# One layer of a chunked hybrid trunk: a shorter mLSTM norm, the bias column negated on ScalarE, and the decay additions queued behind another chunk's norm sum

## The chip, the core and the metric

The kernel runs on one core of a Trainium2 chip. The core has a matrix engine (TensorE, PE in the profile, with its weight loads shown apart as PEld), three engines for elementwise work (VectorE = DVE, ScalarE = ACT, GpSimd = POOL), a queue for data transfers (SyncE = SP) and 16 DMA engines. Each engine takes its instructions in the order of its own queue; an instruction that has to wait holds those behind it. The metric is the time of one execution on the device in microseconds; the median of several runs is compared.

## The reference

One layer over 2048 tokens of width 1024, all in float32. After an RMS norm and one wide projection, three groups of heads work side by side: chunked softmax attention with a relative bias, mLSTM, and gated linear attention (GLA). Their outputs are gated, joined, projected back, added to the input and normalised. What matters here is the end of mLSTM, whose rows are divided by a denominator and then normalised per head, and the relative bias of attention:

```python
# mLSTM, per chunk
d_mat = jnp.exp(log_d - m_row[..., None])            # the decay
sc = jnp.einsum('bnthd,bnjhd->bnhtj', qc, kc) * d_mat
...
den = jnp.maximum(jnp.abs(den), jnp.exp(-m_row))
out = num / den.transpose(0, 1, 3, 2)[..., None]
...
# per head, over 64 columns
y = xf * lax.rsqrt(jnp.mean(xf * xf, axis=-1, keepdims=True) + EPS)
```

## The kernel before

The 2048 tokens are worked off in four quarters of 512 tokens (`q`). In each quarter PE runs the projections: a tile is 24 matmuls of 128x512 into one of two PSUM banks named `ip` (lines L240 to L242 and L260 to L262), which ScalarE or VectorE then evict (L507 to L519, L585 and L586, L490 and L496, and others). Every weight tile arrives by DMA in `wraw` and is split into a high and a low part, by ScalarE (L231) and by VectorE or GpSimd in turn (L232). Between the projections PE does the small matmuls of mLSTM and GLA. After the four quarters (from about 900 us) comes attention with the output projection.

The order of PE's instructions is written out by hand: `Flow` steps through the generators `gates`, `mlstm`, `gla_in`, `gla` and others while the projections run, and each `yield` says how many microseconds of other matmul work should pass before the next step. The order on all other engines is planned by the program that builds the kernel: it simulates the engines and takes, on each, the instruction of highest priority that is ready by its simulation. Evictions and weight splits have a raised priority. The order is then fixed, and on the chip each engine follows it whatever is ready.

A step of `mlstm` is a chunk of 128 tokens, four in a quarter, 16 in all:

- The decay. `load_dd` (L651) loads a row of numbers to all partitions into `dd`, which has two buffers; the load of chunk c+1 is issued in step c and waits for the buffer of chunk c-1. Six additions on VectorE (L665, one for each head, capped by a mask) and one exponential on ScalarE (L667) make the decay.
- The scores. PE multiplies keys by queries (L672), VectorE multiplies by the decay (L684), and PE multiplies by the values (L695).
- The chunk's output, `ov`, is put together on VectorE (L698, L701), with the denominator in column 64 of each head; the state `Cbd` is updated (L716).
- The norm. ScalarE squares the output (L719), VectorE sums the squares (L721) into `sm[:, 0]` and makes the denominator in `sm[:, 1]` (L722 to L724). A reciprocal on VectorE (L725) and five instructions on GpSimd (L726 to L730, the fourth a power of -1/2) make the factor `sm[:, 3]`, all on tiles of 128x6.
- VectorE multiplies the output by the factor (L733), PE transposes it (L631, in `mlstm_out`), and VectorE applies the gate (L633). In the last quarter the transposes of the first three chunks are held back.

GLA has a norm of its own with a power on GpSimd (L892, L893, L895), and a product L853 (after L850) for which PE waits at L860.

`bias_rel`, called once in quarter 1, loads the bias table's last column (L615, `bc`), negates it on VectorE (L616) and adds it to the table `bt` of each of six heads on ScalarE (L619).

Of the kernel before, what the change touches and what calls it, by code (L numbers as in the profile page):

```python
# [1 line left out]

# [8 lines left out]
AF = mybir.ActivationFunctionType  # L11
ALU = mybir.AluOpType
# [12 lines left out]
EPS = 1e-6  # L25
# [80 lines left out]
def trunk_kernel(ctx: ExitStack, tc: tile.TileContext, xT, x, w_f, w_t, w_o, w_gates, norm_g, conv_w,  # L106
                 gate_sel, one_row, bias, ml_g, gla_g, final_g, out):
    nc = tc.nc
# [19 lines left out]
    mhalf = const.tile([P, 16], FP32, name="mhalf")  # L128
# [18 lines left out]
    with ExitStack() as pa_:  # L147
# [13 lines left out]
        def d_tile():  # L161
            return big.tile([P, 6, L], FP32, name="dd", bufs=2)
# [14 lines left out]
        cap = one.tile([P, L], FP32, name="cap")  # L177
# [435 lines left out]
        def bias_rel():  # L613
            bc = big.tile([P, AH], FP32, name="sm")
            nc.sync.dma_start(bc, bias[:, :, 256])  # L615
            nc.vector.tensor_scalar(bc, bc, -1.0, None, op0=ALU.mult)  # L616
            nc.sync.dma_start(bt, bias[:, :, 0:256])
            for h in range(AH):
                nc.scalar.activation(bt[:, h, :], bt[:, h, :], AF.Identity, bias=bc[:, h:h + 1])  # L619
            nc.gpsimd.memset(bt[0:64, :, 192:256], NEG)  # L620
# [24 lines left out]
        def mlstm(q, qk, vs, R, held=None):  # L645
            rt, iwl = R["rt"], R["iwl"]
            if held is not None:
                hbs = [xraws.tile([P, D], FP32, name="xraw") for _ in range(3)][0::2]
            def load_dd(c):
                dd = d_tile()  # L650
                nc.sync.dma_start(dd, nm_d[q, :, c * L:(c + 1) * L].partition_broadcast(P))  # L651
                return dd

            nxt = load_dd(0)
            for c in range(NC):
                t0 = q * QT + c * L
# [4 lines left out]
                dd = nxt  # L661
                if c + 1 < NC:
                    nxt = load_dd(c + 1)
                for e in range(6):
                    nc.vector.scalar_tensor_tensor(dd[:, e, :], dd[:, e, :], rt[:, c, 0, e:e + 1], cap,  # L665
                                                   op0=ALU.add, op1=ALU.min)
                nc.scalar.activation(dd, dd, AF.Exp)  # L667
                yield 0.0, 9.0 if c == 0 else 3.5
                sps = [bank("s", 2) for _ in range(2)]
# [26 lines left out]
                if not first:  # L696
# [3 lines left out]
                                            op=ALU.mult)  # L700
                    nc.vector.tensor_tensor(oc, ov, oc, op=ALU.add)  # L701
                    ov = oc
                if t0 + L < S:
# [5 lines left out]
                    for b in range(2):  # L709
                        r = slice(64 * b, 64 * b + 64)  # L710
                        for a in range(3):
# [3 lines left out]
                            else:  # L715
                                nc.vector.scalar_tensor_tensor(dst, dst, iwl[r, 3 * b + a, c:c + 1], cv[r, a, :],  # L716
                                                               op0=ALU.mult, op1=ALU.add)
                sq = m_tile([P, 2, 3, 64])
                nc.scalar.activation(sq, ov[:, :, :, 0:64], AF.Square)  # L719
                sm = big.tile([P, 4, 2, 3], FP32, name="sm")  # L720
# [1 line left out]
                nc.vector.tensor_scalar(sm[:, 1], ov[:, :, :, 64], -1.0, None, op0=ALU.mult)  # L722
                nc.vector.tensor_tensor(sm[:, 1], sm[:, 1], rt[:, c, 2, :].rearrange("p (b a) -> p b a", b=2), op=ALU.max)
                nc.vector.tensor_tensor(sm[:, 1], ov[:, :, :, 64], sm[:, 1], op=ALU.max)  # L724
                nc.vector.reciprocal(sm[:, 1], sm[:, 1])  # L725
                nc.gpsimd.tensor_tensor(sm[:, 2], sm[:, 1], sm[:, 1], op=ALU.mult)  # L726
                nc.gpsimd.tensor_tensor(sm[:, 2], sm[:, 2], sm[:, 0], op=ALU.mult)
                nc.gpsimd.tensor_scalar(sm[:, 2], sm[:, 2], 1.0 / 64, EPS, op0=ALU.mult, op1=ALU.add)
                nc.gpsimd.tensor_tensor(sm[:, 2], sm[:, 2], mhalf[:, 0:6].rearrange("p (b a) -> p b a", b=2), op=ALU.pow)
                nc.gpsimd.tensor_tensor(sm[:, 3], sm[:, 2], sm[:, 1], op=ALU.mult)  # L730
                late_ = held is not None and c < NC - 1
                hb = m_tile([P, 3, 2, 64]) if held is None else hbs[c // 2][:, 512 * (c % 2):512 * (c % 2) + 384].rearrange("p (a b d) -> p a b d", a=3, b=2)
                nc.vector.tensor_tensor(hb.rearrange("p a b d -> p b a d"), ov[:, :, :, 0:64],  # L733
# [173 lines left out]
        for q in range(NQ):  # L907
# [3 lines left out]
            if q == NQ - 1:  # L911
                z = proj_z(X)
                G, gh, mh = {}, [], []
                tail = proj_v(X)
                vs, vg = next(tail)
                flow.start("gla_in", gla_in(q, z, R, G))
                flow.need("mlstm")
                qk = proj_m(X)
                flow.need("gates")
                st["per"] = 2  # L920
                M = dict(R)
                flow.start("mlstm", mlstm(q, qk, vs, M, mh))
                flow.start("mlstm_out", held_out(q, mh, M))
                gg = proj_gg(X)
                next(tail)
                flow.start("gla", gla(q, vg, gg, G, gh))
                flow.start("gla_out", held_gla(q, lambda: gg, gh))
                M["gm"] = proj_gm(X)
                proj_a(q, X)
                break  # L930
# [12 lines left out]
            if q == 1:  # L943
                bias_rel()
            M = dict(R)
            flow.start("mlstm", mlstm(q, qk, vs, M))
            M["gm"] = proj_gm(X)
            R = {}
# [391 lines left out]
```

## Time and profile before

| | us |
|---|---|
| median of 3 runs | 1302.21 (1302.17 to 1312.29) |
| the profiled execution | 1304.63 |
| its span, first to last instruction | 1302.5 |

The median is that of three executions without the profiler. The profiled execution is another one; all rows are of it, in microseconds from its first instruction. A row of the timeline has start, duration, engine, line, operation, output and inputs by their names in the program, shape, and in brackets the idle time of that engine just before, with the instruction that ended it. A row of waits names who waited for whom, the sum, how often, and the longest. A row of a stretch has, for each engine, busy time and number of instructions, then the granted clock of TensorE (1.00 is full speed), the share of time in which the DMA engines were busy, and the rate of transfers in GB/s.

### The profile page before, as it was taken

The page shows a single profiled execution, that of the slowest core. Times are in us where ns is not written, and L with a number is a line of the kernel's source. Part 1 is how long each engine was busy: PE and PEld are TensorE (multiplying, and loading weights), DVE is VectorE, ACT ScalarE, POOL GpSimd, SP SyncE. Part 2 cuts the span into 40 slices and gives each one's busy share as a digit, 9 for nine tenths or more (in the row PEclk, how much of TensorE's full clock was granted, in tenths as well). Part 3 has the DMA queues.
Part 4 walks back from the last instruction along what each step waited for, and adds up shares of the span by engine and source line. Part 5 has one row for each costly group of instructions (what it writes and reads, how often), then busy time and mean ns, then how long its engine had stood idle before and what let it go on. Part 6 is the DMA issues. An engine that isn't in the chain of part 4 may idle for free.

```text
span 1302.5 us, 19360 instructions
## 1 busy us (share of the span) xinstructions
PE 1254.7 (96%) x6804; PEld 1021.0 (78%) x6804; DVE 800.8 (61%) x1838; ACT 590.2 (45%) x1096; POOL 604.3 (46%) x825
## 2 busy tenths in 40 slices
PE   8989999999999999999999999999988999999997
PEld 7867877878787788878778877787867878878876
DVE  6646645772575668267476766664567677666631
ACT  5536332453533236353323643332565566655631
POOL 3337663233766243375533455652354454554432
PEclk8989999999999999999999999999989999999999
DMA  6147344424733442473344242426785565655322
GB/s 226 57 135 255 98 140 128 119 55 139 255 97 111 124 128 72 138 254 92 113 126 126 75 135 89 131 59 191 231 231 188 184 191 161 190 173 176 97 90 81
DMA packets 100185, 184.34 MB, mean 142 GB/s; under 512 B 10592, under 2 KB 46304, under 8 KB 100088
## 3 DMA queue, kind: packets, MB, share of 16 engines
q1 hardware_dynamic: 95624, 174.98, 43.2%
q10 hardware_dynamic: 4464, 8.13, 1.7%
q8 instruction: 53, 0.87, 0.3%
q14 instruction: 44, 0.36, 0.1%
HBM read 147.38 MB, written 35.70 MB: 141 GB/s over the span
## 4 chain that ended last, share of the span: by engine, by line
PE 72%; DVE 9%; DMA 7%; POOL 4%; ACT 3%; issue 3%; SPq 0%; POOLq 0%; DVEq 0%; ACTq 0%
PE ip L240 10%; PE ip L242 10%; PE ip L241 10%; PE ip L1192 4%; PE ip L1194 4%; PE ip L1193 4%; PE s L1051 3%; PE ip L260 3%; PE tp L1111 3%; PE ip L262 3%; PE ip L261 3%; DMA wraw<-in_w_f 2%; DMA dd<-nm_d 2%; PE ga L843 2%; PE w L1130 2%
## 5 line engine op out<-in xcount | busy, mean ns | idle before, releaser
L240 PE MATMUL ip<-x,w 128*128 128x512 f32 x784 | 321.4, 410 | 1.4 <-ACT u L551 1.4
L242 PE MATMUL ip<-x,w 128*128 128x512 f32 x784 | 308.3, 393 | 0.0
L241 PE MATMUL ip<-x,w 128*128 128x512 f32 x784 | 307.4, 392 | 0.0
L240 PEld LDWEIGHTS ip<-x,w 128*128 128x128 f32 x784 | 148.5, 189 | 43.3 <-issue 11.7
L242 PEld LDWEIGHTS ip<-x,w 128*128 128x128 f32 x784 | 148.0, 189 | 32.7
L241 PEld LDWEIGHTS ip<-x,w 128*128 128x128 f32 x784 | 148.8, 190 | 29.3 <-issue 1.9
L231 ACT CAST w<-wraw 128x1024 fp32r<-128x1024 f32 x126 | 131.6, 1046 | 64.9 <-DMA wraw<-in_w_f 33.5
L232 POOL TENSOR_TENSOR w<-wraw,w 128x1024 fp32r<-128x1024 f32 x42 | 103.9, 2473 | 111.7 <-ACT w L231 111.6
L232 DVE TENSOR_TENSOR w<-wraw,w 128x1024 fp32r<-128x1024 f32 x84 | 111.3, 1325 | 64.6 <-ACT w L231 64.5
L1072 POOL TENSOR_SCALAR pt<-pt,sm 128x640 f32<-128x640 f32 (+2 forms) x96 | 71.4, 746 | 112.2 <-DVE sm L1071 90.2
L260 PE MATMUL ip<-w,x 128*128 128x512 f32 x256 | 104.3, 407 | 8.2 <-DVE e L496 5.5
L262 PE MATMUL ip<-w,x 128*128 128x512 f32 x256 | 101.3, 396 | 0.0
L261 PE MATMUL ip<-w,x 128*128 128x512 f32 x256 | 101.1, 395 | 0.0
L1070 ACT ACTIVATE pt<-pt,sm 128x640 f32<-128x640 f32 (+2 forms) x96 | 73.2, 763 | 47.1 <-DVE sm L1067 43.4
L786 POOL TENSOR_TENSOR prd<-gk,zg 128x16 f32<-128x16 f32 (+7 forms) x112 | 66.5, 594 | 58.6 <-PE pw L792 53.3
L1118 DVE TENSOR_TENSOR pl<-tp,ph 128x512 fp32r<-128x512 f32 (+1 forms) x108 | 71.9, 673 | 33.1 <-ACT ph L1117 32.8
L1051 PE MATMUL s<-kk,qq 128*128 128x256 f32 (+2 forms) x360 | 83.8, 318 | 7.6 <-DVE sm L1067 2.8
L1051 PEld LDWEIGHTS s<-kk,qq 128*128 128x128 f32 x360 | 63.5, 192 | 22.7 <-DVE sm L1067 7.6
L783 POOL TENSOR_TENSOR gk<-gk,al 128x16 f32<-128x16 f32 (+14 forms) x120 | 70.8, 590 | 21.3 <-ACT al L760 14.3
L1117 ACT CAST ph<-tp 128x512 fp32r<-128x512 f32 (+1 forms) x108 | 60.5, 572 | 42.2 <-PE tp L1111 41.5
L560 DVE SCALAR_TENSOR_TENSOR qk<-u,cw,qk 128x512 f32<-128x512 f32 x72 | 68.4, 950 | 13.7 <-ACT qk L558 12.1
L1201 POOL TENSOR_TENSOR xr<-xr,e 128x512 f32<-128x512 f32 x31 | 40.1, 1293 | 60.8 <-ACT jk L1199 60.5
(345 smaller groups left out, 2481.6 us busy)
## 6 DMA issues: line engine op xcount, KB each, us to landing
wraw<-in_w_f SPq DMA_DIRECT2D x100, 512.0 KB, 3.7
wraw<-in_w_t SPq DMA_DIRECT2D x28, 512.0 KB, 3.7
qq<-q_d SPq DMA_DIRECT2D x48, 256.0 KB, 4.9
kk<-k_d SPq DMA_DIRECT2D x18, 512.0 KB, 6.3
vv<-v_d SPq DMA_DIRECT2D x18, 512.0 KB, 5.9
xraw<-in_xT SPq DMA_DIRECT2D x16, 512.0 KB, 6.1
xr<-in_x SPq DMA_DIRECT2D x16, 512.0 KB, 3.6
out<-xr ACTq DMA_DIRECT2D x31, 256.0 KB, 2.6
```

The costliest lines, as they stand in the source:

```text
L231: nc.scalar.copy(w[:, :, 0, :], rv)
L232: other().tensor_tensor(w[:, :, 1, :], rv, f32(w[:, :, 0, :]), op=ALU.subtract)
L240: nc.tensor.matmul(ps, w[:, k, 0, :], X[k][:, 0, :], start=(k == 0), stop=False)
L241: nc.tensor.matmul(ps, w[:, k, 0, :], X[k][:, 1, :], start=False, stop=False)
L242: nc.tensor.matmul(ps, w[:, k, 1, :], X[k][:, 0, :], start=False, stop=(k == KT - 1))
L260: nc.tensor.matmul(ps, X[k][:, 0, t], w[:, 0, :], start=(k == 0), stop=False)
L261: nc.tensor.matmul(ps, X[k][:, 0, t], w[:, 1, :], start=False, stop=False)
L262: nc.tensor.matmul(ps, X[k][:, 1, t], w[:, 0, :], start=False, stop=(k == KT - 1))
L1051: nc.tensor.matmul(sp[:, :cn], qq[:, l, tt * P:(tt + 1) * P], kk[:, ko + c0:ko + c0 + cn], start=(l == 0), stop=(l == 1))
L1070: nc.scalar.activation(pt[:, :n], pt[:, :n], AF.Exp, bias=init, scale=-1.0, accum_out=sm[:, 2:3])
L1072: nc.gpsimd.tensor_scalar(pt[:, :n], pt[:, :n], sm[:, 3:4], 0.5, op0=ALU.mult, op1=ALU.mult)
L1118: nc.vector.tensor_tensor(pl[:, :w], tp[:, :w], f32(ph[:, :w]), op=ALU.subtract)
```

## The change

Three edits. The negation of the bias column goes from VectorE to ScalarE. The norm of mLSTM is written without a reciprocal: where n is the denominator and s the sum of 64 squares, the factor (1/n) (s/(64 n²) + EPS)^(-1/2) becomes (s/64 + EPS n²)^(-1/2), with two VectorE instructions and one power on GpSimd. And the six decay additions of a chunk are put behind the second of these two instructions, the norm sum, of the chunk before it in the same quarter: `tc.issue_after(behind)` gives the planner an edge from that instruction to those traced in the block, on the same engine, without a semaphore. The first chunk of each quarter has none.

```diff
         def bias_rel():
             bc = big.tile([P, AH], FP32, name="sm")
             nc.sync.dma_start(bc, bias[:, :, 256])
-            nc.vector.tensor_scalar(bc, bc, -1.0, None, op0=ALU.mult)
+            nc.scalar.activation(bc, bc, AF.Copy, scale=-1.0)
...
+            behind = None
             nxt = load_dd(0)
             for c in range(NC):
...
                 for e in range(6):
-                    nc.vector.scalar_tensor_tensor(dd[:, e, :], dd[:, e, :], rt[:, c, 0, e:e + 1], cap,
-                                                   op0=ALU.add, op1=ALU.min)
+                    with tc.issue_after(behind) if behind else nullcontext():
+                        nc.vector.scalar_tensor_tensor(dd[:, e, :], dd[:, e, :], rt[:, c, 0, e:e + 1], cap,
+                                                       op0=ALU.add, op1=ALU.min)
...
-                nc.vector.reciprocal(sm[:, 1], sm[:, 1])
-                nc.gpsimd.tensor_tensor(sm[:, 2], sm[:, 1], sm[:, 1], op=ALU.mult)
-                nc.gpsimd.tensor_tensor(sm[:, 2], sm[:, 2], sm[:, 0], op=ALU.mult)
-                nc.gpsimd.tensor_scalar(sm[:, 2], sm[:, 2], 1.0 / 64, EPS, op0=ALU.mult, op1=ALU.add)
-                nc.gpsimd.tensor_tensor(sm[:, 2], sm[:, 2], mhalf[:, 0:6].rearrange("p (b a) -> p b a", b=2), op=ALU.pow)
-                nc.gpsimd.tensor_tensor(sm[:, 3], sm[:, 2], sm[:, 1], op=ALU.mult)
+                nc.vector.scalar_tensor_tensor(sm[:, 2], sm[:, 1], EPS, sm[:, 1], op0=ALU.mult, op1=ALU.mult)
+                behind = nc.vector.scalar_tensor_tensor(sm[:, 2], sm[:, 0], 1.0 / 64, sm[:, 2], op0=ALU.mult, op1=ALU.add).ins
+                nc.gpsimd.tensor_tensor(sm[:, 3], sm[:, 2], mhalf[:, 0:6].rearrange("p (b a) -> p b a", b=2), op=ALU.pow)
```

More of the change, by code (lines that the diff above doesn't have):

```diff
@@ L1 @@
-from contextlib import ExitStack
+from contextlib import ExitStack, nullcontext
 import concourse.bass as bass
```

## The prediction

> **What bounds the kernel.** I read the page's first part first: who is busy for how long. TensorE (PE) is busy for 96% of the span, the other engines for 45 to 61%. So time can come only out of the 4% in which PE stands still, and out of stretches in which it runs at a lower clock. An engine beside PE matters only where PE waits for it.
>
> ```profile
> span 1302.5 us, 19360 instructions
> PE 1254.7 (96%) x6804; PEld 1021.0 (78%) x6804; DVE 800.8 (61%) x1838; ACT 590.2 (45%) x1096; POOL 604.3 (46%) x825
> ```
>
> Then the timeline of PE, for rows with idle time in front. Between 75 and 900 us, where the mLSTM chunks run, five gaps of about 2 us or more have their cause beside the edited lines. The bracket tells the idle time and who ended it.
>
> ```profile
> 211.36 0.33 PE L631 MATMUL mt<-ident,m 128*128 128x128 f32 x1 [1.93 <-DVE m L733]
> 279.16 0.50 PE L260 MATMUL ip<-w,x 128*128 128x512 f32 x1 [2.38 <-ACT vg L519]
> 444.30 0.90 PE L631 MATMUL mt<-ident,m 128*128 128x128 f32 x3 [2.05 <-DVE m L733]
> 674.23 0.55 PE L631 MATMUL mt<-ident,m 128*128 128x128 f32 x3 [2.63 <-DVE m L733]
> 845.52 0.48 PE L860 MATMUL ga<-Sbd,q 128*128 128x256 f32 x1 [2.36 <-DVE at L853]
> ```
>
> Three times PE waits for L733, the product of the chunk's output with the norm's factor; once for L853, GLA's; once for L519, an eviction on ScalarE (ACT). Together 1.93+2.38+2.05+2.63+2.36 = 11.35 us.
>
> The third view gives each engine's busy time in stretches of 8 us that begin with those gaps; the first number after POOL's bracket is the granted TensorE clock.
>
> ```profile
> 209.43:217.43 8.00, 6.07 (x22) 4.89 (x22) 1.72 (x3) 1.53 (x2) 3.09 (x3) 0.79 0.57 129
> 276.78:284.78 8.00, 5.62 (x18) 4.43 (x18) 5.19 (x26) 4.94 (x12) 4.75 (x16) 0.79 0.41 101
> 442.25:450.25 8.00, 5.95 (x22) 4.91 (x22) 3.18 (x5) 1.53 (x2) 1.24 (x3) 0.79 0.48 112
> 671.60:679.60 8.00, 5.37 (x26) 4.50 (x26) 3.18 (x5) 1.53 (x2) 1.82 (x3) 1.00 0.50 143
> 843.16:851.16 8.00, 5.64 (x28) 4.60 (x29) 7.87 (x17) 3.05 (x5) 5.44 (x8) 0.79 0.20 63
> ```
>
> Four of the five gaps cost twice: the clock over the 8 us is 0.79, so 0.21 x 8 = 1.7 us of matmul time goes once the work has come back. After the gap at 671.60 the clock stays at 1.00. So the five stalls cost 11.35 + 4 x 1.7 = 18.15 us, 1.4% of the span.
>
> The Trainium skill, page "TensorE: Matmul & The Clock Gate", Part 1, section "What's actually happening", has the clock fall to half only after an idle window of about 3.4 us, on a free-running window. By it these gaps of 1.9 to 2.6 us would cost only themselves, and the sum would be 11.35 us. The rows disagree (0.79 after gaps of 1.93 to 2.38 us), and agree with it only in that the longest gap, 2.63 us, can go free; the measurement decides.
>
> **The tie of the decay additions.** The cause of a stall stands in VectorE's (DVE) rows before it. Here is the one at 444.30.
>
> ```profile
> 435.54 1.67 DVE L665 SCALAR_TENSOR_TENSOR dd<-dd,rt,cap 128x128 f32<-128x128 f32 x6 [1.37 <-DMA dd<-nm_d]
> 438.93 0.54 DVE L721 TENSOR_REDUCE sm<-m 128x6 f32<-128x384 f32 x1
> 439.67 0.15 DVE L724 TENSOR_TENSOR sm<-m,sm 128x6 f32<-128x6 f32 x1
> 439.86 0.19 DVE L725 RECIPROCAL sm<-sm 128x6 f32<-128x6 f32 x1
> 443.36 0.42 DVE L895 TENSOR_TENSOR n<-ga,sm 128x256 f32<-128x256 f32 x1 [2.39 <-POOL sm L893]
> 443.70 0.55 DVE L733 TENSOR_TENSOR m<-m,sm 128x384 f32<-128x384 f32 x1
> ```
>
> The six additions are those of chunk 3, two chunks ahead. DVE takes its instructions in order and stands 1.37 us for their DMA, then works 1.67 us on them, while the norm of chunk 1 is queued behind: 3.04 us. After the edit they may only follow the norm sum of chunk 2. That takes 3.04 us from this path, against the 2.05 us that PE waited: the stall goes even if nothing else helps. The other places:
>
> ```profile
> 201.39 1.67 DVE L665 SCALAR_TENSOR_TENSOR dd<-dd,rt,cap 128x128 f32<-128x128 f32 x6
> 210.15 0.69 DVE L586 SCALAR_TENSOR_TENSOR hl<-ip,hl 128x512 fp32r<-128x512 f32 x1 [1.65 <-ACT hl L585]
> 664.46 3.50 DVE L665 SCALAR_TENSOR_TENSOR dd<-dd,rt,cap 128x128 f32<-128x128 f32 x6 [0.91 <-DMA dd<-nm_d]
> 839.48 4.35 DVE L665 SCALAR_TENSOR_TENSOR dd<-dd,rt,cap 128x128 f32<-128x128 f32 x6 [3.43 <-DMA dd<-nm_d]
> 843.85 0.88 DVE L850 TENSOR_TENSOR at<-gb,msk 128x128 f32<-128x128 f32 x4
> ```
>
> At 664.46, 0.91+3.50 = 4.41 us leave the path against a gap of 2.63. At 839.48, 3.43+4.35 = 7.78 us stand ahead of L850 and so of L853, against 2.36. At 201.39 only 1.67 us leave, against 1.93; that alone is not enough, and the shorter norm has to give the rest. So the tie should clear three stalls for certain and a fourth with help: 2.05+1.7, 2.63, 2.36+1.7, 1.93+1.7.
>
> What the tie adds is a wait for the additions themselves. Behind them hang ACT's exponential and the score product, and PE after that. Before, the additions were waiting for data:
>
> ```profile
> DVE dd L665 <- DMA dd<-nm_d: 16.5, 7, 3.4
> ACT dd L667 <- DVE dd L665: 30.7, 11, 6.4
> 835.69 0.19 DVE L725 RECIPROCAL sm<-sm 128x6 f32<-128x6 f32 x1
> 838.97 0.94 PE L672 MATMUL s<-qk 64*128 64x128 f32 x12
> 845.38 1.01 DVE L684 TENSOR_TENSOR dd<-s,dd 128x384 f32<-128x384 f32 x2
> L667 ACT ACTIVATE dd<-dd x16: 837/845/849, 78.4 to 843.9; 128x768 f32<-128x768 f32 x16
> ```
>
> The tightest tied chunk is chunk 2 of the last quarter: the norm of chunk 1 ends at 835.9, the scores at 838.97+0.94 = 839.9. Additions (1.67) and exponential (0.85) end 2.5 us after the norm, at 838.4, 1.5 us before the scores and 7 us before the product ran. If that cover were gone, each late microsecond would be one of PE. The DMA for dd is issued as before, on the same condition (its buffer), so SP's queue keeps its order; the 16.5 us in which DVE stood for it lose what was queued behind. DVE's 96 additions are moved, not removed; between norm sum and L733 they may lie in DVE's way, between nothing and one set (1.67 us) late. I take nothing: DVE is idle there while GpSimd works (2.39 us in the row at 443.36).
>
> **The shorter norm.** GpSimd's rows at the same place:
>
> ```profile
> 440.13 0.20 POOL L726 TENSOR_TENSOR sm<-sm 128x6 f32<-128x6 f32 x1 [9.40 <-DVE sm L725]
> 441.03 1.32 POOL L729 TENSOR_TENSOR sm<-sm,mhalf 128x6 f32<-128x6 f32 x1
> 442.32 1.01 POOL L893 TENSOR_TENSOR sm<-sm,mhalf 128x4 f32<-128x4 f32 x1
> 443.29 0.20 POOL L730 TENSOR_TENSOR sm<-sm 128x6 f32<-128x6 f32 x1
> ```
>
> Before, from the end of L724 (439.82) to the start of the power 1.21 us pass, and L730 adds 0.20 behind it. After, two DVE instructions of 128x6 stand in between. No row has this form; bounds are L724's 0.15 and the reciprocal's 0.19, so I take 0.17 each, and the same hop to GpSimd (0.08). 1.21+0.20 becomes 0.34+0.08 = 0.42: about 1.0 us a chunk, and GLA's power L893 no longer stands between the mLSTM's power and its last product. At 201.39, 1.67+1.0 = 2.7 us exceed the gap of 1.93. The busy sums, 16 x (0.34-0.19) = +2.4 us on DVE and some 16 x 0.8 = -13 us on GpSimd, are off the path and cost nothing.
>
> **The bias column.** ACT's rows before the stall at 279.16:
>
> ```profile
> 274.45 0.53 ACT L719 ACTIVATE m<-m 128x384 f32<-128x384 f32 x1
> 277.67 0.91 ACT L619 ACTIVATE bt<-bt,sm 128x256 f32<-128x256 f32 x2 [2.70 <-DVE sm L616]
> 278.86 0.25 ACT L519 COPY vg<-ip 128x128 f32<-128x128 f32 x1
> 269.82 0.60 SPq L615 DMA_DIRECT2D sm<-in_bias  x1
> DMA to landing us min/median/max: 3.6/3.6/3.6
> ```
>
> ACT stands 2.70 us for a DVE instruction of six columns that is late in DVE's queue, and L519, which gives PE its bank back, stands behind. The data was there at 269.82+3.6 = 273.4. On ACT the column costs between nothing and a small copy (0.25, L519's row); I take 0.2. 2.70-0.2 = 2.5 us exceed the gap of 2.38, so the stall goes: 2.38+1.7 us. If all six bias additions now come ahead of L519 (four more of 0.45), up to 1.8 us of it stays.
>
> **The sum.** All five: 18.15 us. But the program plans each engine's order anew, except PE's, and PE reaches later waits up to 18 us sooner than work that it doesn't pace; I give back one stall of average size, 18.15/5 = 3.6 us. The gain is 14.5 us. The profiled execution took 1304.6 us (its span and 2.1 around it) and would take 1290.1; the median of the runs is 1302.2, so I forecast 1287.7.
>
> **The rivals.**
> (a) Another instruction takes the head of the queue. At 210.15 L586 waits for ACT's L585 ahead of L733. If that order stays, and comes at the other two as well, the norm is ready earlier but leaves DVE no sooner, and the three stalls at L631 stay; only those at 279.16 and 845.52 go: 8.2 us, 1294.0. For it: the row at 210.15. Against: at 444.30 and 674.23 no such row stands in front.
> (b) The clock falls less often than four times in five, as 671.60 shows it can: only the gaps count, 11.35 less one average (2.3), 1293.1. Against: four of five. The skill's 3.4 us, on the page named above, would make this the rule.
> (c) The change doesn't do what it says: new orders bring as many stalls as go; about 1302.
> (d) Slower. The exponential holds ACT. ACT takes in order too, and the exponential of the twelve tied chunks now hangs on a norm sum in the same queue as evictions that PE needs. Where the sum is later than planned, ACT stands, and PE with it, at 2.38+1.7 = 4.1 us as at 279.16. From 18.15/4.1, five of the twelve, it loses; at eight, 1302.2-18.15+32.8 = 1316.9. For it: ACT stood 30.7 us for these additions already. Against: DVE itself stood 16.5 us for the DMA there, which goes.
>
> **How the numbers follow.** Forecast 0.60, its own range 1283 to 1294; (a) 0.15; (b) 0.05; (c) 0.12; (d) 0.08. The range 1281 to 1304 leaves out (d), half of (c)'s spread above 1302 and a little under 1283. A measurement of this kernel can tell about 1%, 13 us, so faster means under 1289.2: four fifths of the forecast, 0.48, and 0.02 of the rest: 0.50. Slower is (d), 0.08; the same 0.42.
>
> **What would show it.** Right: no idle time of DVE at the additions of chunks 1 to 3; L631 and L860 without their four gaps; ACT without 2.70 us before L619; one GpSimd instruction per norm; a clock of 1.00 where 0.79 stood. Wrong: a gap at L631 whose row ahead on DVE is L586; ACT idle before the exponential with an eviction behind it; new gaps of 2 us at other lines.

## The result, and the profile after

| | before | after |
|---|---|---|
| median of 4 runs each, us | 1302.85 | 1291.31 |
| lowest to highest, us | 1302.17 to 1312.29 | 1291.09 to 1291.62 |
| the profiled execution, us | 1304.63 | 1291.09 |
| its span, us | 1302.5 | 1289.4 |

The changed kernel takes 0.9895 of the time before, with a 95% interval of 0.985 to 0.994: 11.5 us less. The prediction was 1287.7 us, a gain of 14.5. Line numbers shift: the additions L665 are now L667, the exponential L667 is L669, the norm sum is L728, the power L729, the product L733 is L732, GLA's L853 is L852 and PE's L860 is L859.

The page's first part, after:

```profile
span 1289.4 us, 19320 instructions
PE 1249.2 (97%) x6804; PEld 1018.4 (79%) x6804; DVE 799.4 (62%) x1853; ACT 590.1 (46%) x1097; POOL 589.0 (46%) x761
```

GpSimd lost 15 us of work, DVE and ACT kept theirs within 1.5 us, and PE is busy for 5.5 us less with the same 6804 matmuls. As before, what counts is where PE stands still and at what clock it runs. The timeline of PE at the five places of the prediction, and at one more:

```profile
211.57 0.27 PE L631 MATMUL mt<-ident,m 128*128 128x128 f32 x1
...
276.70 0.50 PE L260 MATMUL ip<-w,x 128*128 128x512 f32 x1 [1.40 <-ACT vg L519]
...
437.32 0.27 PE L631 MATMUL mt<-ident,m 128*128 128x128 f32 x1
...
662.76 0.27 PE L631 MATMUL mt<-ident,m 128*128 128x128 f32 x1
...
786.40 0.50 PE L260 MATMUL ip<-w,x 128*128 128x512 f32 x1 [2.57 <-DVE e L496]
...
834.00 0.38 PE L859 MATMUL ga<-Sbd,q 128*128 128x256 f32 x1
```

Three transposes at L631 and the matmul at L859 have no bracket: no idle time stands in front. At L260 1.40 of 2.38 us stay. And at 786.40 PE waits 2.57 us for the product L496, which it did for 1.03 us at the same matmul before.

The stretches of 8 us there: at the eviction's wait, at two of the transposes, and at the new wait:

```profile
273.90:281.90 8.00, 6.60 (x30) 5.09 (x29) 6.65 (x29) 4.65 (x12) 4.86 (x13) 1.00 0.36 91
435.30:443.30 8.00, 8.00 (x40) 6.54 (x38) 3.08 (x6) 1.66 (x3) 1.01 (x1) 1.00 0.47 109
660.70:668.70 8.00, 8.00 (x39) 6.54 (x38) 4.03 (x9) 2.90 (x5) 1.01 (x1) 1.00 0.42 99
783.80:791.80 8.00, 5.43 (x26) 4.04 (x25) 3.76 (x5) 2.65 (x4) 4.81 (x6) 0.79 0.37 131
```

PE's first number was 5.4 to 6.1 us of 8.00 at the five gaps before; at the transposes it is now all 8.00, at a granted clock of 1.00. At the eviction it is 6.60, but the clock stays at 1.00. The 0.79 has moved to the new wait.

Both kernels issue the same 6804 matmuls in the same order, so the start of any one can be subtracted, after minus before. The difference changes in steps, and each step has a place:

| where, by before's time | step, us |
|---|---|
| start, up to 75 us (clock) | +2.15 |
| 211.36, L631 | -3.6 |
| 279.16, L260 behind L519 | -2.6 |
| 356.73, L240 behind L551 | -0.7 |
| 444.30, L631 | -3.8 |
| 674.23, L631 | -2.9 |
| 796.42, L260 behind L496 | +3.1 |
| 818.18 | -0.6 |
| 845.52, L860 | -4.15 |
| attention, from 900 us | 0.0 |
| sum | -13.1 |

The spans differ by 1289.4 - 1302.5 = -13.1. Two steps go the wrong way: the first, where nothing was changed, and the one at L496. The first is a matter of the clock, as the same stretch of both kernels shows (before, then after):

```profile
18.40:26.40 8.00, 8.00 (x40) 6.05 (x44) 8.00 (x11) 6.22 (x9) 5.38 (x3) 1.00 0.54 194
```

```profile
18.90:26.90 8.00, 8.00 (x27) 6.45 (x28) 8.00 (x11) 6.18 (x9) 5.35 (x3) 0.76 0.49 179
```

PE is busy for all 8.00 us in both, but gets 27 matmuls done in place of 40, at 0.76. The other engines have the same work in it. Whether that belongs to the change is the first experiment.

### The profile page after: what moved, and what is told of

It is laid out like the page before. It is cut to its first block, busy times and chain, and to the rows that moved or that the text cites. A ratio compares the mean times of both kernels' runs of the same rounds, so it can differ in the third digit from the quotient of the medians.

```text
span 1289.4 us, 19320 instructions
## 1 busy us (share of the span) xinstructions
PE 1249.2 (97%) x6804; PEld 1018.4 (79%) x6804; DVE 799.4 (62%) x1853; ACT 590.1 (46%) x1097; POOL 589.0 (46%) x761
## 4 chain that ended last, share of the span: by engine, by line
PE 79%; DVE 6%; DMA 5%; POOL 3%; ACT 3%; issue 3%; SPq 0%; POOLq 0%; ACTq 0%; DVEq 0%
PE ip L240 12%; PE ip L242 11%; PE ip L241 11%; PE ip L260 4%; PE ip L1191 4%; PE ip L1193 4%; PE ip L261 4%; PE ip L1192 4%; PE ip L262 4%; PE s L1050 3%; PE tp L1110 3%; PE ga L842 2%; DVE qk L560 2%; PE w L1129 2%; PE w L1126 2%
## 5 line engine op out<-in xcount | busy, mean ns | idle before, releaser
L240 PE MATMUL ip<-x,w 128*128 128x512 f32 x784 | 319.6, 408 | 0.7 <-ACT u L551 0.7
L240 PEld LDWEIGHTS ip<-x,w 128*128 128x128 f32 x784 | 147.3, 188 | 42.2 <-issue 10.6
L231 ACT CAST w<-wraw 128x1024 fp32r<-128x1024 f32 x126 | 131.6, 1046 | 59.2 <-DMA wraw<-in_w_f 29.6
L260 PE MATMUL ip<-w,x 128*128 128x512 f32 x256 | 103.9, 406 | 8.9 <-DVE e L496 7.5
L560 DVE SCALAR_TENSOR_TENSOR qk<-u,cw,qk 128x512 f32<-128x512 f32 x72 | 70.2, 975 | 15.4 <-ACT qk L558 13.9
L490 ACT ACTIVATE e<-ip 128x512 f32<-128x512 f32 x44 | 26.2, 595 | 94.4 <-PE ip L242 85.4
```

What stands on the lines that cost most here:

```text
L231: nc.scalar.copy(w[:, :, 0, :], rv)
L240: nc.tensor.matmul(ps, w[:, k, 0, :], X[k][:, 0, :], start=(k == 0), stop=False)
L260: nc.tensor.matmul(ps, X[k][:, 0, t], w[:, 0, :], start=(k == 0), stop=False)
L560: nc.vector.scalar_tensor_tensor(acc, zb[:, i:i + QT], cw[:, b, i:i + 1], acc, op0=ALU.mult, op1=ALU.add)
```

## The experiments

Every run is compared with runs of the kernel before on the same chip. Those had medians of 1305.75 us (first group of four runs below: again, no_tie, no_norm, no_bias), 1303.61 (second: only_bias, tie_but_one, bias_later, best), 1303.57 (third: tie_c1, tie_last2) and 1303.95 (fourth: again_5, but_one_5). Short diffs are against the kernel after. This table is worked out from the profiled execution of each: the idle time of PE, in us, in front of the same matmul of the fixed order (A, B, C are the transposes L631, E is L260 behind L519, L496 is L260 behind that line, D is L860 before and L859 after; places in before's time).

| kernel | A 211 | E 279 | L551 357 | B 444 | C 674 | L496 796 | D 846 |
|---|---|---|---|---|---|---|---|
| before | 1.93 | 2.38 | 1.38 | 2.05 | 2.63 | 1.03 | 2.36 |
| after | 0 | 1.40 | 0.68 | 0 | 0 | 2.57 | 0 |
| again | 0 | 1.40 | 0.68 | 0 | 0 | 2.70 | 0 |
| again_5 | 0 | 1.40 | 0.53 | 0 | 0 | 2.39 | 0 |
| no_tie | 0.45 | 1.40 | 0.01 | 0 | 0.28 | 0 | 2.68 |
| no_norm | 0 | 1.41 | 0.93 | 0 | 0 | 2.62 | 0 |
| no_bias | 0 | 2.37 | 0 | 0 | 0 | 2.44 | 0 |
| only_bias | 1.93 | 1.41 | 0.36 | 1.03 | 2.59 | 1.29 | 2.56 |
| tie_but_one | 0 | 1.40 | 0.68 | 0 | 0 | 0 | 0 |
| bias_later | 0 | 0 | 0.99 | 0 | 0 | 2.43 | 0 |
| best | 0 | 0 | 1.07 | 0 | 0 | 0 | 0 |
| tie_c1 | 0.68 | 1.41 | 0 | 0 | 0.28 | 2.72 | 1.90 |
| tie_last2 | 0.47 | 1.41 | 0.40 | 0.02 | 0.28 | 1.11 | 0 |
| but_one_5 | 0 | 1.40 | 1.41 | 0 | 0 | 0 | 0 |

**again: the kernel after, unaltered.** It asks whether the lost clock at the start, and the wait at L496, come back.

> The changed kernel once more, unaltered. Expected 1291.3 us within 0.5. Theory 1 says that the 2.2 us by which its first 75 us were longer than before's come from the phase in which the clock comes back (matmuls at about 20 us running at half clock), not from the change: then another execution can have that stretch at full clock, 2 us shorter. Rival: it belongs to the program, and the matmuls from 18.9 us on are at half clock again. The gap of 2.57 us at L260 near 786 us should come back in both.

Measured: 1290.70 us (4 runs, 1289.67 to 1291.89), ratio 0.9888 (0.9870 to 0.9906). The stretch at the start, and the wait:

```profile
18.60:26.60 8.00, 7.96 (x36) 6.05 (x40) 8.00 (x10) 6.26 (x9) 5.37 (x3) 1.00 0.53 190
```

```profile
784.53 0.50 PE L260 MATMUL ip<-w,x 128*128 128x512 f32 x1 [2.70 <-DVE e L496]
```

The clock at the start is 1.00 here with the same kernel: the 2.15 us are not the change's. The wait at L496 is there in both, and so belongs to it.

**no_tie: the additions are not tied.** Norm and bias column as changed.

```diff
-                behind = nc.vector.scalar_tensor_tensor(sm[:, 2], sm[:, 0], 1.0 / 64, sm[:, 2], op0=ALU.mult, op1=ALU.add).ins
+                nc.vector.scalar_tensor_tensor(sm[:, 2], sm[:, 0], 1.0 / 64, sm[:, 2], op0=ALU.mult, op1=ALU.add)
```

> The changed kernel with the additions not tied; norm and bias column stay as changed. Theory 1 (the tie does most of the work): the stalls at L631 in quarters 1 and 2 and the one at L860 in quarter 3 come back, 3.8+2.6+4.1 = 10.5 us, about 1301.8. Rival (the shorter norm is enough for L631, because the power no longer waits behind three products nor GLA's power ahead of the last one, some 2 us against gaps of 2): only the stall at L860 comes back, about 1295.4.

Measured: 1291.89 us (1288.81 to 1295.10), ratio 0.9897 (0.9870 to 0.9924): the time of the kernel after. Both the 1301.8 of my theory and the 1295.4 of its rival lie above it. PE at the four places that the tie was to clear:

```profile
210.18 0.33 PE L631 MATMUL mt<-ident,m 128*128 128x128 f32 x1 [0.45 <-DVE m L732]
...
435.28 0.27 PE L631 MATMUL mt<-ident,m 128*128 128x128 f32 x1
...
661.50 0.33 PE L631 MATMUL mt<-ident,m 128*128 128x128 f32 x1 [0.28 <-DVE m L732]
...
831.45 0.48 PE L859 MATMUL ga<-Sbd,q 128*128 128x256 f32 x1 [2.68 <-DVE at L852]
```

Without the tie the transposes wait 0.45, 0 and 0.28 us in place of 1.93, 2.05 and 2.63. Only GLA's matmul has its gap back, as the rival had it. What it didn't foresee is that the wait at L496 goes (0 in the table). So the tie brings one stall's cure and one new stall, and the transposes are cured by something else as well.

**no_norm: the old norm, with the tie.** The tie hangs on the reciprocal, the last VectorE instruction of the old norm.

```diff
-                nc.vector.scalar_tensor_tensor(sm[:, 2], sm[:, 1], EPS, sm[:, 1], op0=ALU.mult, op1=ALU.mult)
-                behind = nc.vector.scalar_tensor_tensor(sm[:, 2], sm[:, 0], 1.0 / 64, sm[:, 2], op0=ALU.mult, op1=ALU.add).ins
-                nc.gpsimd.tensor_tensor(sm[:, 3], sm[:, 2], mhalf[:, 0:6].rearrange("p (b a) -> p b a", b=2), op=ALU.pow)
+                behind = nc.vector.reciprocal(sm[:, 1], sm[:, 1]).ins
+                nc.gpsimd.tensor_tensor(sm[:, 2], sm[:, 1], sm[:, 1], op=ALU.mult)
...
```

> The changed kernel with the old norm (reciprocal, five GpSimd instructions), additions tied behind the reciprocal of the chunk before; bias column as changed. Theory 1: the tie alone clears the stalls in quarters 1, 2 and 3; in quarter 0 it takes 1.67 us from a gap of 1.93, so 0.3 us stay: 1291.3 to 1293. Rival (the tied additions now lie between reciprocal and L733, and the long norm has no slack left): gaps of about 2 us at L631 again in three quarters, about 1300.

Measured: 1293.11 us (1289.49 to 1295.26), ratio 0.9903 (0.9880 to 0.9927). All three transposes are without a gap, the first too, which by the prediction needed the shorter norm's help. The tie alone clears them.

**only_bias: the old norm and no tie.** Neither cure, beside the bias column.

```diff
-                nc.vector.scalar_tensor_tensor(sm[:, 2], sm[:, 1], EPS, sm[:, 1], op0=ALU.mult, op1=ALU.mult)
-                behind = nc.vector.scalar_tensor_tensor(sm[:, 2], sm[:, 0], 1.0 / 64, sm[:, 2], op0=ALU.mult, op1=ALU.add).ins
-                nc.gpsimd.tensor_tensor(sm[:, 3], sm[:, 2], mhalf[:, 0:6].rearrange("p (b a) -> p b a", b=2), op=ALU.pow)
+                nc.vector.reciprocal(sm[:, 1], sm[:, 1])
+                nc.gpsimd.tensor_tensor(sm[:, 2], sm[:, 1], sm[:, 1], op=ALU.mult)
...
```

> Of the three edits only the bias column on ScalarE; old norm, no tie. Theory 2 (formed after the kernel without the tie: at L631 tie and shorter norm are two cures of the same stalls, either is enough): with both gone the three stalls at L631 and the one at L860 are back, each 2 to 2.6 us with a slow clock behind most of them; only the 2.6 us at 277 and 0.7 at 352 are won: about 1299. Rival (those stalls went by the new order that any edit brings): about 1292.

Measured: 1300.13 us (10 runs, 1298.07 to 1307.28), ratio 0.9988 (0.9970 to 1.0006).

```profile
213.82 0.33 PE L631 MATMUL mt<-ident,m 128*128 128x128 f32 x1 [1.93 <-DVE m L735]
...
441.99 0.33 PE L631 MATMUL mt<-ident,m 128*128 128x128 f32 x1 [1.03 <-DVE m L735]
...
672.32 0.47 PE L631 MATMUL mt<-ident,m 128*128 128x128 f32 x1 [2.59 <-DVE m L735]
...
845.01 0.48 PE L862 MATMUL ga<-Sbd,q 128*128 128x256 f32 x1 [2.56 <-DVE at L855]
```

With neither, all four are back, the second at half its size. So tie and shorter norm are two cures of the same three stalls, each enough by itself but for 0.45 and 0.28 us, and leaving out either one says nothing about what it is worth.

**no_bias: the column is negated on VectorE again.**

```diff
-            nc.scalar.activation(bc, bc, AF.Copy, scale=-1.0)
+            nc.vector.tensor_scalar(bc, bc, -1.0, None, op0=ALU.mult)
```

> The changed kernel with the bias column negated on VectorE as before. Theory 1: the gap at L260 near 277 us goes from 1.40 us with full clock back to 2.4 us with a clock of about 0.79 behind it: 2.6 us, about 1293.9. Rival (what was gained there is lost later, since the conv chain and not PE sets the time before 786 us): the gap there shrinks instead, and the time stays at 1291.3.

Measured: 1294.12 us (1293.53 to 1297.68), ratio 0.9923 (0.9899 to 0.9947), 3.4 us above again in the same group. The gap at E is as before, so the rival, by which it shrinks, falls:

```profile
277.29 0.50 PE L260 MATMUL ip<-w,x 128*128 128x512 f32 x1 [2.37 <-ACT vg L519]
```

The 3.4 us are not all the column's. The profiled executions of the two (1293.53 and 1290.27) differ by 3.3, of which 1.9 us come at the start, where the clock was 1.00 in again. At E no_bias loses 0.97, with the clock at 1.00 behind the gap, and it has 0.7 of that back at L551.

What the edit left of that gap, 1.40 us, has its reason in ACT's rows of the kernel after:

```profile
273.39 0.19 ACT L616 ACTIVATE sm<-sm 128x6 f32<-128x6 f32 x1
273.62 2.51 ACT L619 ACTIVATE bt<-bt,sm 128x256 f32<-128x256 f32 x6
276.03 0.47 ACT L517 ACTIVATE v<-ip 128x384 f32<-128x384 f32 x1
276.40 0.25 ACT L519 COPY vg<-ip 128x128 f32<-128x128 f32 x1
```

ACT no longer stands for the column, but now all six additions of the bias come ahead of the eviction, where before only two did.

**bias_later: the call of `bias_rel` moved behind the start of the next two generators.**

```diff
             flow.need("gates")
-            if q == 1:
-                bias_rel()
             M = dict(R)
...
             flow.start("prep", prep(q + 1, R, dg))
+            if q == 1:
+                bias_rel()
             proj_a(q, X)
```

> The changed kernel with the bias step moved behind the gates of quarter 1, just ahead of the attention projections. Theory 2: the 1.40 us that stay at L260 near 277 are the six bias additions ahead of the eviction L519; elsewhere on ACT they stand ahead of nothing that is due, so this gap goes, 1.4 us less, about 1289.9. Rival (ACT is late there because it waited for VectorE's scans, and the additions only fill that time): the gap stays.

Measured: 1288.64 us (1286.44 to 1289.99), ratio 0.9885 (0.9868 to 0.9902). The eviction L519 comes ahead of the six additions, and E has no gap. A gain of 1.4 us is too small for these intervals: the trace shows it, the times don't.

**tie_but_one: no tie for chunk 1 of the last quarter.** The wait at L496 stands in the last quarter, and goes with the tie. In the kernel after, the order of ACT's rows from the first L551 to the wait (first fence) differs from before (second) in one place:

```profile
744.57 0.57 ACT L551 COPY u<-ip 128x512 f32<-128x512 f32 x1
746.46 1.05 ACT L231 CAST w<-wraw 128x1024 fp32r<-128x1024 f32 x1 [1.32 <-DMA wraw<-in_w_f]
747.42 0.71 ACT L558 ACTIVATE qk<-u,cw 128x512 f32<-128x512 f32 x1
```

```profile
757.37 0.58 ACT L551 COPY u<-ip 128x512 f32<-128x512 f32 x1
757.98 0.72 ACT L558 ACTIVATE qk<-u,cw 128x512 f32<-128x512 f32 x1
759.72 1.05 ACT L231 CAST w<-wraw 128x1024 fp32r<-128x1024 f32 x1 [1.02 <-DMA wraw<-in_w_f]
```

L551, L558, three products on DVE (L560), L562 and L563 are a convolution, six times in a row, with one buffer `u` between them. In the kernel after the split of a weight tile (L231) comes between L551 and L558, and ACT stands 1.32 us there for the tile's DMA, with the convolution behind it: L558 starts 2.85 us after L551, where before it was 0.61. The convolutions follow one another on that buffer, and L496 stands behind the last: it starts 41.1 us after the first L551, in place of 38.3 before, and PE waits for it. What moved the split was to be found among the tied additions near by, those of chunk 1:

```diff
-                    with tc.issue_after(behind) if behind else nullcontext():
+                    with tc.issue_after(behind) if behind and (q, c) != (NQ - 1, 1) else nullcontext():
```

> The changed kernel with one of the twelve ties taken out, that of chunk 1 in the last quarter. Theory 2: with that tie the exponential of chunk 1 left its place on ACT near 735 us, the plan then put a weight split L231 ahead of the conv's first product L558, it stands for its DMA, the chain of conv products starts later, and PE waits 2.57 us for L496 near 786 with the clock at half behind it. Without that tie L558 stands ahead again: no such gap there, and the stall at L860 stays cured, 2.6+1.6 = 4.2 us less than the changed kernel, about 1287. Rival (PE waits there because it comes earlier by what was won before, whatever ACT's order): the gap stays at 2.5 us, about 1291.

Measured: 1286.66 us (1283.83 to 1288.27), ratio 0.9875 (0.9857 to 0.9893). ACT has the old order again, and PE no wait:

```profile
742.63 0.58 ACT L551 COPY u<-ip 128x512 f32<-128x512 f32 x1
743.24 0.72 ACT L558 ACTIVATE qk<-u,cw 128x512 f32<-128x512 f32 x1
744.78 1.05 ACT L231 CAST w<-wraw 128x1024 fp32r<-128x1024 f32 x1 [0.81 <-DMA wraw<-in_w_f]
...
781.67 0.51 PE L260 MATMUL ip<-w,x 128*128 128x512 f32 x1
```

**tie_c1: this one tie alone.** With norm and bias as changed, and every other tie left out.

```diff
-                    with tc.issue_after(behind) if behind else nullcontext():
+                    with tc.issue_after(behind) if behind and (q, c) == (NQ - 1, 1) else nullcontext():
```

> Norm and bias column as changed, and of the twelve ties only that of chunk 1 in the last quarter. Theory 2: this one tie is enough to bring the gap of about 2.6 us at L260 <- L496 near 785 us, which the kernel without ties did not have, with a slow clock behind it; the gap at L860 (2.7 us without ties) stays, since chunks 2 and 3 are not tied: 4 us more than without ties, about 1295.5. Rival (several ties together make that order): no gap at L496, about 1291.5.

Measured: 1298.71 us (7 runs, 1295.25 to 1304.81), ratio 0.9963 (0.9937 to 0.9989), against 0.9897 without any tie. That is 3.2 us above what I expected; of the 7.2 us between the profiled executions of this kernel and no_tie 4.4 lie at L496, the rest is spread.

```profile
785.23 0.50 PE L260 MATMUL ip<-w,x 128*128 128x512 f32 x1 [2.72 <-DVE e L496]
...
835.64 0.48 PE L859 MATMUL ga<-Sbd,q 128*128 128x256 f32 x1 [1.90 <-DVE at L852]
```

One tie of twelve is enough for the wait at L496, and with no other it costs more than it gives. So the wait at its full size, 2.4 to 2.7 us, comes with this tie alone (tie_c1) and goes when only this one is left out (tie_but_one). A wait of 1.0 to 1.3 us at the same matmul comes without it too: before, only_bias and the next run have one.

**tie_last2: ties only in the last quarter, without that of chunk 1.**

```diff
-                    with tc.issue_after(behind) if behind else nullcontext():
+                    with tc.issue_after(behind) if behind and q == NQ - 1 and c > 1 else nullcontext():
```

> Norm and bias column as changed, ties only for chunks 2 and 3 of the last quarter (two of twelve). Theory 2: the shorter norm alone holds the three waits at L631 to 0.5 us or less, the two ties cure L860, and the gap at L496 does not come: 1286.7 of the kernel with eleven ties plus 0.7, about 1287.4. Rival (the other nine ties are worth the 3.8+2.6 us of the stalls that they cured): about 1292.

Measured: 1288.60 us (1286.60 to 1291.02), ratio 0.9883 (0.9856 to 0.9910). GLA's stall is cured by these two ties alone, and the transposes wait 0.47 and 0.28 us as without a tie. A miss: at L496 1.11 us stay, about what the kernel before has there (1.03), though L558 comes ahead of the late split. So ACT's order is not all that holds L496 back. In this run the first three products of the convolution meet a weight split on GpSimd:

```profile
747.25 4.35 DVE L560 SCALAR_TENSOR_TENSOR qk<-u,cw,qk 128x512 f32<-128x512 f32 x3
748.66 2.40 POOL L232 TENSOR_TENSOR w<-wraw,w 128x1024 fp32r<-128x1024 f32 x1 [1.38 <-ACT w L231]
```

They take 4.35 us, where they take 2.33 in tie_but_one (from 744.00), and L496 starts 39.5 us after the first L551, in place of 38.3. The kernel after has such a meeting as well: 3.94 us from 748.16, beside a split at 747.59. So what its convolution loses at the start is 2.24 us by ACT's order and up to 1.6 by this meeting; no run parts the two. Nor is it the whole account: before and only_bias wait at L496 with 2.33 us for these products.

**again_5 and but_one_5: after and tie_but_one side by side, in more runs.** The same two kernels, unaltered.

> The changed kernel unaltered, timed beside the next on the same chip, for a direct comparison: 1291 us, with the gap of about 2.6 us at L260 <- L496 near 785 us.

> The changed kernel without the tie of chunk 1 in the last quarter, timed beside the one before. Theory 2: 4.2 us less than it, about 1287, and no gap at L496. Rival (the earlier difference was the scatter of the clock, some 2 us at each stall): within 1.5 us of it.

Measured: 1291.38 us (1288.29 to 1292.40) and 1287.39 (1286.96 to 1287.87), ratios 0.9897 (0.9881 to 0.9914) and 0.9869 (0.9851 to 0.9888). By the medians the one tie costs 1291.38 - 1287.39 = 4.0 us; the theory had 4.2. Without it the slowest run (1287.87) is faster than the fastest run with it (1288.29), though the intervals of the ratios overlap a little. In the profiled execution of again_5 the clock stayed at 1.00 behind the wait, and the step there is 2.7 us alone.

**best: tie_but_one and bias_later together.** Both edits as above.

> Both at once: one tie out, bias step moved. Theory 2: 1291.3 - 4.2 - 1.4 = about 1285.7. Rival: no better than the changed kernel, 1291, because the freed time is lost at the next wait.

Measured: 1287.80 us (1286.63 to 1292.39), ratio 0.9887 (0.9864 to 0.9909). That is 2.1 us above what I expected. Both gaps are gone, and it isn't measurably faster than tie_but_one. In attention a matmul waits 5.15 us for a load, where the kernel after waits 2.88 and tie_but_one 3.90:

```profile
956.01 0.98 PE L1050 MATMUL s<-kk,qq 128*128 128x384 f32 x2 [5.15 <-DMA wraw<-y_d]
```

That the one comes from the other was not tried. The lowest median is that of tie_but_one, some 4 us under the kernel after; the intervals of best, bias_later and tie_last2 overlap its by more than half, so no order among these four is shown.

## Why the prediction was nearly right

**Bound and price of a stall: right.** The steps at A, B, C and D are -3.6, -3.8, -2.9 and -4.15 us; the prediction had 3.6 (1.93 + 1.7), 3.75, 2.63 and 4.06. Both are measured against the same execution of the kernel before, with the clock as it fell there; the last section shows that another execution can pay the 1.7 us at other gaps.

**The tie: the effect right, its part overstated.** It put A, B, C and D down to the tie, A with the shorter norm's help. The tie does clear all four (no_norm). But the shorter norm clears A to C by itself too, to 0.45, 0 and 0.28 us (no_tie), and only D needs the tie. The step that misled is the norm's price, "about 1.0 us a chunk". DVE in no_tie, at B:

```profile
432.27 0.16 DVE L726 TENSOR_TENSOR sm<-m,sm 128x6 f32<-128x6 f32 x1
...
434.27 0.56 DVE L732 TENSOR_TENSOR m<-m,sm 128x384 f32<-128x384 f32 x1 [0.50 <-POOL sm L729]
435.24 0.42 DVE L894 TENSOR_TENSOR n<-ga,sm 128x256 f32<-128x256 f32 x1 [0.42 <-POOL sm L892]
```

From the denominator's last step to the product are 434.27 - 432.27 = 2.00 us. Before they were 443.70 - 439.67 = 4.03. So the kernel with the shorter norm has 2.03 us less here, and the gap went down by 2.05. The same two lines give 1.48 us at A (gap 1.48 less) and 2.35 at C (gap 2.35 less). The other microsecond at B is GLA's: its product L895 and its power of 1.01 us stood ahead of L733, and now its product stands behind. The prediction named that ("GLA's power L893 no longer stands between") and didn't add it. At A it was L586, which stood 1.65 us in front of the product and now comes after it.

The cover for the tied additions held. DVE stood 16.5 us for their DMA before. After it is 0.7, and ACT's wait for them fell from 30.7 to 11.1:

```profile
ACT dd L669 <- DVE dd L667: 11.1, 10, 4.6
DVE dd L667 <- DMA dd<-nm_d: 0.7, 1, 0.7
```

What they cost between the norm sum and the product, which the prediction took as nothing, is seen at A (VectorE, and GpSimd's power):

```profile
206.12 0.17 DVE L727 SCALAR_TENSOR_TENSOR sm<-sm 128x6 f32<-128x6 f32 x1
206.32 0.17 DVE L728 SCALAR_TENSOR_TENSOR sm<-sm 128x6 f32<-128x6 f32 x1
206.40 1.66 DVE L667 SCALAR_TENSOR_TENSOR dd<-dd,rt,cap 128x128 f32<-128x128 f32 x6
206.56 1.36 POOL L729 TENSOR_TENSOR sm<-sm,mhalf 128x6 f32<-128x6 f32 x1 [6.33 <-DVE sm L728]
...
208.70 0.55 DVE L732 TENSOR_TENSOR m<-m,sm 128x384 f32<-128x384 f32 x1
```

They fill the time in which GpSimd works on the power: the power ends at 207.92, the additions at 208.06. Three short instructions of GLA that come next move the product on to 208.70, some 0.7 us late. That cost PE nothing, since it comes to the transpose only at 211.57. The two new instructions take 0.17 us each, as taken.

**The bias column: a size off.** The copy took 0.19 us (0.2 taken). Of 2.38 + 1.7 = 4.1 us it gave 2.6, 1.0 by the gap and 1.6 by the clock, which no_bias shows can stay at 1.00 behind the same gap. The case "if all six bias additions now come ahead of L519 ... up to 1.8 us of it stays" came, with 1.40.

**What is given back: the size right, the reason wrong.** The prediction gave back one average stall, 3.6 us, because "PE reaches later waits up to 18 us sooner than work that it doesn't pace". Given back were 3.1 us between the profiles (4.0 between the medians of again_5 and but_one_5), but not to later waits in general: over attention as a whole nothing was given back (0.0). That an average stall of 3.6 met it in size is luck. What came was one new order. The tie of chunk 1 in the last quarter moved its additions, a weight split came ahead of a convolution's first product on ACT, and PE waits for L496 at the end of that chain. That this tie brings the full wait is shown both ways. The steps between are read from the rows: the split was not moved by itself, and its meeting with the products on VectorE has a part that wasn't measured.

**The sum.** Of the 18.15 us foreseen 1.5 stayed at E and 3.1 were given back; 1.3 came on top at L551 and at 818, and 0.4 at the other four. That is 15.25 us, of which the clock at the start took 2.15 in this execution: 13.1. The forecast was 14.5. Beside the medians of the later groups (1305.75 and 1303.95) the kernel after gains 15.0 and 12.6 us; the 1302.21 from which it started was at the low end of what before takes.

**The rivals.** (a) L586 did not keep the head of the queue at A: the product L732 runs at 208.70, 0.8 us behind the power and with no L586 ahead of it, and no transpose waits. (b) That only gaps count: the steps at A, B and D are too large for it. (c) New orders did come, but brought one stall, not five. With it one of the signs of being wrong that the prediction named came, a new gap of 2 us at another line. (d) ACT's wait for the additions fell, and no eviction that PE needed was held by an exponential.

## What to carry to other kernels

Where a planner lays out the queues, an edit's price is not read off its own instructions alone: compare the new order of every engine for some microseconds behind each moved instruction, above all for transfers that an in-order engine now waits for ahead of a chain that PE needs. Where two edits cure the same stall, leaving out one of them shows next to nothing; it takes a run without both to see what they are worth. And an order that is imposed at twelve places should be tried place by place: here one of the twelve cost 4 us, and two others were enough for the stall that the shorter norm left standing.

## What the runs showed of the hardware

**The price of a gap scatters.** PE's gap at E was 2.38 us in the kernel before and 2.37 in no_bias. Behind the first the granted clock was 0.79 over 8 us, behind the second (and behind the 2.39 us at L496 in again_5):

```profile
275.00:283.00 8.00, 5.71 (x26) 4.69 (x27) 5.15 (x27) 4.94 (x12) 3.65 (x12) 1.00 0.49 101
```

```profile
780.00:788.00 8.00, 5.61 (x34) 4.14 (x34) 5.21 (x7) 2.65 (x4) 5.01 (x8) 1.00 0.37 102
```

it was 1.00. At C it was the other way round: 1.00 behind 2.63 us before, 0.79 behind 2.59 in only_bias. So the 1.7 us behind a stall come or don't come with the execution, as at the start (0.76 and 1.00 with one kernel), and single executions of one kernel differ by some 2 us for each place. The Trainium skill, page "TensorE: Matmul & The Clock Gate", Part 1, section "What's actually happening", says that the window in which activity is counted runs freely and that the number of slow matmuls varies from run to run. The runs agree with that. They don't agree with its idle window of about 3.4 us, since gaps of 1.93 to 2.57 us were followed by 0.79.

**VectorE beside GpSimd.** In the kernel before the six additions at 839.48 took 4.35 us in place of 1.67, since one of them took 2.48 while GpSimd ran a weight split. First the group by its tile (minimum, median and maximum, in ns, of the 24 in the last quarter), then the timeline of GpSimd:

```profile
L665 DVE SCALAR_TENSOR_TENSOR dd<-dd,rt,cap x24: 340/348/2481, 745.4 to 843.5; 128x128 f32<-128x128 f32 x24
```

```profile
839.58 2.50 POOL L232 TENSOR_TENSOR w<-wraw,w 128x1024 fp32r<-128x1024 f32 x1
```

The same is seen ahead of the wait at L496 after, where three products took 4.35 us with a median of 0.77 each (timeline of the kernel after, VectorE and GpSimd):

```profile
780.01 4.35 DVE L560 SCALAR_TENSOR_TENSOR qk<-u,cw,qk 128x512 f32<-128x512 f32 x3
...
780.48 2.54 POOL L232 TENSOR_TENSOR w<-wraw,w 128x1024 fp32r<-128x1024 f32 x1 [0.26 <-ACT w L231]
```

In both places the instruction of DVE that met the split lasted about as long as it, seven times its own usual time in the first (2.48 and 0.35 us) and 3.6 times in the second (2.77 and 0.77). The Trainium skill, page "GPSIMD Engine Reference", section "1. Specifications", says that GpSimd shares its memory interfaces with VectorE, with contention for VectorE instructions that have two inputs there. The rows agree; no run here was made to try it by itself.
